# The entry of the MLP: a norm tile's stores moved from ACT's queue to POOL's, and the first raw weights fetched in a step of their own

## The chip, the core and the metric

One core of one Trainium2 chip runs the kernel. The metric is the device time of one execution in microseconds (us), and smaller is better. The engines are named as the profile names them: PE (TensorE, matmuls), ACT (ScalarE), DVE (VectorE), POOL (GpSimd), SP (SyncE, which here only issues DMAs). ACT, SP and POOL each have a queue through which they can start DMAs. An engine takes its own instructions strictly in order, a DMA start among them.

## What is computed

One block of a diffusion transformer over 2048 tokens of 1024 channels: a token mixer (Fourier and neighbourhood attention, gated), and then a dense MLP with 4096 hidden channels. The change touches the place where the second begins.

```python
x = x + g1 * mixed
hx2 = modulate(rms_norm(x, norm2_g[l]), sh2, sc2)
x = x + g2 * sqrelu_mlp(hx2, w_mlp1[l], w_mlp2[l])

def sqrelu_mlp(h, w1, w2):
    a = jax.nn.relu(h @ w1)
    return (a * a) @ w2
```

## The kernel before

Every float32 operand is split into two float16 halves (high and low), and a product of two is three matmuls. The MLP's two matrix products are done as 2x2 block products in the Strassen-Winograd form: seven products of sums of blocks instead of eight. The tokens run in two halves of 1024.

**Up to the MLP.** `out_proj(t, i)` (L1400 on) makes the mixer's output for 128 tokens, adds x, stores the sum to `x1d` through SP's queue and normalises it. `norm_T(t)` (L1420 on) transposes 256 normalised tokens (`tpb`), makes `tm`, and then seven sums of its blocks. For each of the seven, `put` (L1440 on) lets ACT write the high half of a tile `ho` (L1442) and DVE the low half (L1443), and stores it to `hcd` (L1444). The order is 0, 5, 6, 4, 3, 2, 1. There are four `ho` buffers: the fifth, sixth and seventh put wait until the stores of the first three have landed. There are eight tiles t; those of t = 4 to 7 go to `hcd[1]`, which is read when the second half of the tokens begins. Tiles 6 and 7 are stored through ACT's queue, all others through SP's.

**The MLP's operands.** Half 0 reads `hcd[0]` as seven tiles `hc`, 1 MB each, through SP's queue (L1503). Four of them (products 0, 5, 6, 4) are loaded early. The other three (1, 3, 2) live in space (`pr`) that the mixer's output stage (`pg`) held until then; their load is written after `norm_T(7)`.

**The MLP's weights.** They too must be made into seven block sums each, as float16 halves, in DRAM. `prepare` (L383 on) does it for a list of jobs, one job for 256 rows or columns: it fetches a raw weight of 1 MB (`fetch`, L387; here through ACT's queue), and then takes seven steps. Each step has up to one sum on DVE (L423), a high half on ACT (L380) and a low half on DVE (L381), and a store (`flush`, L398; here through POOL's queue). The second step fetches the next raw weight. Eight of the 32 jobs are done far ahead, beside the input projections, by the same generator (`early_blocks`, L367 on; there through SP's queue). The other 24, 168 steps, run beside the MLP's first half. In the loop at the end of the kernel each slot (one product of a unit of the first matrix, or a group of products of the second) adds its cost to `done`, and steps are taken as long as `steps * horizon < done * todo`. `horizon` is the summed cost of the slots within which all must be done: 732, so that a slot of cost 4 takes 4 x 168 / 732 = 0.92 step.

**The MLP's products.** `mlp1(half, f)` yields after each of seven products in the order 0, 5, 6, 4, 1, 3, 2 (`PRODUCTS`). A product is 12 matmuls into one of four PSUM buffers; DVE's sums (`plus`, L1546) and ACT's copies, relus and squares (`acts`, L1550) read it and free the buffer. The first four products of the first unit are written ahead of `norm_T(7)`; the loop starts with the fifth (`if i > 3`).

Within these rules the order of each engine's instructions is set by a scheduler that simulates the program at build time; at run time each engine keeps to that order and waits on semaphores. A DMA of SP's or ACT's queue counts its end on one of eight semaphores, taken in turn by both queues together, and before a DMA is started on such a semaphore the earlier DMA on it must have landed. POOL's queue has eight semaphores of its own.

Of the kernel before, what the change touches and what calls it, by code (L numbers as in the profile page):

```python
# [63 lines left out]
def dit_block(ctx: ExitStack, tc: tile.TileContext, a, out, taps=None, upto=9):  # L64
    nc = tc.nc
    act, dve, pool, pe, sp = nc.scalar, nc.vector, nc.gpsimd, nc.tensor, nc.sync
# [312 lines left out]
    def halve(hi, lo, src, scale):  # L379
        act.activation(hi, src, AF.Copy, scale=scale)  # L380
        dve.scalar_tensor_tensor(out=lo, in0=src, scalar=scale, in1=hi, op0=ALU.mult, op1=ALU.subtract)  # L381

    def prepare(todo, raw_room, sum_room, out_room, n_out, load_, dma):  # L383

        todo, raws, out_, room = list(todo), {}, [], []

        def fetch(n):  # L387
            if n < len(todo):
                kind, f = todo[n]
                raws[n] = t = raw_room(f"raw{kind}_{f}")  # L390
                if kind == 1:
                    load_(t.rearrange("p (k n) -> p k n", k=KT), a["w_mlp1"][0, :, f * 128:(f + 2) * 128].rearrange("(k p) n -> p k n", p=128))
                else:
                    load_(t.rearrange("p (k n) -> p k n", k=2), a["w_mlp2"][0, f * 128:(f + 2) * 128, :].rearrange("(k p) n -> p k n", p=128))

        def flush():
            while out_:
                dma(*out_.pop(0))  # L398

        fetch(0)  # L400
        for n, (kind, f) in enumerate(todo):
            t, nm = raws.pop(n), f"{kind}_{f}"
            if kind == 1:
                t = t.rearrange("p (k n) -> p k n", k=KT)
                b11, b12, b21, b22 = (t[:, 4 * k:4 * k + 4, i * 128:(i + 1) * 128] for i in range(2) for k in range(2))
            else:
                b11, b12, b21, b22 = (t[:, i * 512:(i + 1) * 512] for i in range(4))
            sums = sum_room(f"ws{nm}")
            s3 = sums.rearrange("p (k n) -> p k n", k=4) if kind == 1 else sums

            def put(j, src):

                if j % n_out == 0:
                    flush()
                    room[:] = [out_room(f"wo{nm}_{j}")]
                    end = min(j + n_out, 7)
                    out_.append(((w1d, w2d)[kind - 1][f // 2][j:end].rearrange("c p n -> p c n"), room[0][:, :end - j]))
                o = room[0][:, j % n_out].rearrange("p (o n) -> p o n", o=2)
                d = o.rearrange("p o (k n) -> p o k n", k=4) if kind == 1 else o
                halve(d[:, 0], d[:, 1], src, msc[:, 0:1] if kind == 1 else msc[:, 2:3])  # L420

            def total(o, x, y, op=ALU.subtract):
                dve.tensor_tensor(out=o, in0=x, in1=y, op=op)  # L423
                return o

            if kind == 1:
                order = ((b11, ()), (s3, (b21, b22, ALU.add)), (s3, (s3, b11)), (b12, ()), (b21, (b11, b21)), (b22, ()), (s3, (b12, s3)))
            else:
                order = ((b11, ()), (s3, (b12, b11)), (s3, (b22, s3)), (b22, ()), (b12, (b22, b12)), (b21, ()), (s3, (b21, s3)))
            for j, (o, ops) in enumerate(order):  # L430
                if ops:
                    total(o, *ops)
                put(j, o)
                if j == 0 and n:
                    prepared.add(todo[n - 1])
                if j == 1:
                    fetch(n + 1)
                yield
        flush()
        prepared.add(todo[-1])  # L440
# [979 lines left out]
    def norm_T(t, q_=sp):  # L1420


        tm = pg.tile([128, KT, 2, 128], F32, tag="tm", name=f"tm{t}")
        x0, x1 = (normed.pop((t, i)) for i in range(2))
        for q in range(4):
            tp = tpp.tile([128, 2, 2, 128], F32, tag="tp", name=f"tpb{t}_{q}")
            for j in range(2):
                k = 2 * q + j
                for i, xh in enumerate((x0, x1)):
                    pe.transpose(tp[:, j, i], xh[:, k * 128:(k + 1) * 128], ident)  # L1430
            for j in range(2):
                k = 2 * q + j
                bi, sc = AB2[:, k:k + 1], AB2[:, 8 + k:9 + k]
                if j:
                    dve.tensor_scalar(out=tm[:, k], in0=tp[:, j], scalar1=sc, scalar2=bi, op0=ALU.mult, op1=ALU.add)
                else:
                    act.activation(tm[:, k], tp[:, j], AF.Identity, bias=bi, scale=sc)
        b11, b12, b21, b22 = (tm[:, 4 * k:4 * k + 4, i] for k in range(2) for i in range(2))

        def put(c, src):  # L1440
            o = pg.tile([128, 2, 4, 128], F16, tag="ho", name=f"ho{t}_{c}", bufs=4)
            act.activation(o[:, 0], src, AF.Copy)  # L1442
            dve.tensor_tensor(out=o[:, 1], in0=src, in1=o[:, 0], op=ALU.subtract)  # L1443
            q_.dma_start(hcd[t // 4][c, :, t % 4], o.rearrange("p o k t -> p (o k t)"))  # L1444

        def total(c, x, y, out=None):
            if out is None:
                out = pg.tile([128, 4, 128], F32, tag="hs", name=f"hs{t}_{c}", bufs=2)
            dve.tensor_tensor(out=out, in0=x, in1=y, op=ALU.subtract)
            return out  # L1450

        t1 = total(4, b12, b11)
        t2 = total(5, b22, t1)
        put(0, b11)
        put(5, t2)
        total(6, b22, b12, b12)
        put(6, b12)
        put(4, t1)
        put(3, total(3, b21, t2))
        put(2, b22)  # L1460
        put(1, b21)
# [37 lines left out]
    def load_hc(half, part, then=None):  # L1499
        r = {}  # L1500
        for c in (PRODUCTS[:4], PRODUCTS[4:])[part]:
            r[c] = (pr if part else pl).tile([128, 4, 2, 4, 128], F16, tag=f"hc{c}", name=f"hc{half}_{c}")
            i = sp.dma_start(r[c].rearrange("p s o k t -> p s (o k t)"), hcd[half][c])  # L1503
        if then:

            then[0] = i
        return r
# [11 lines left out]
    def blocks_of(s):  # L1519
        return [s] if s[0] == 1 else [(2, s[1], f, s[3]) for f in s[5]]  # L1520
# [8 lines left out]
    def load_block():  # L1529
        b = next(stream, None)  # L1530
        if b is None:
            return
        kind, half, f, c = b
        while (kind, f) not in prepared:
            next(prep)
        wbs[b] = t = pl.tile([128, 2, 512], F16, tag="wb", name=f"wb{kind}_{half}_{f}_{c}", bufs=RING)
        with tc.issue_after(ring_load[0].ins) if ring_load[0] else nullcontext():
            ring_load[0] = sp.dma_start(t.rearrange("p o n -> p (o n)"), (w1d, w2d)[kind - 1][f // 2][MADE[kind].index(c)])
# [72 lines left out]
    t = NT - 2  # L1611
# [8 lines left out]
    units[0, 0] = mlp1(0, 0)  # L1620
    for _ in range(4):
        next(units[0, 0])
    norm_T(t + 1, act)
    if taps and "x1" in taps:
        sp.dma_start(taps["x1"], x1d)
    for p_ in (pg, tpp):
# [10 lines left out]
    def small(name):  # L1637
        return pr.tile([128, 512], F32, tag="wo", name=name, bufs=5)

    prep = prepare(jobs, lambda n_: pr.tile([128, 2048], F32, tag="raw", name=n_, bufs=2), lambda n_: pr.tile([128, 512], F32, tag="wt", name=n_),  # L1640
                   lambda n_: small(n_).bitcast(F16).rearrange("p (c n) -> p c n", c=1), 1, act.dma_start, pool.dma_start)
    acc, banks = {}, {}
# [80 lines left out]

    todo, steps, done = 7 * len(jobs), 0, 0
    cost = [4 if s[0] == 1 else len(s[5]) for s in slots]
    horizon = sum(cost[:next(i for i, s in enumerate(slots) if s[:4] == (2, 0, NF - GF, 0)) - RING])
    for i, s in enumerate(slots):
        anchors = dict(last)
        if s[0] == 1:
            _, half, f, c = s  # L1730
            if (half, f) not in units:
                units[half, f] = mlp1(half, f)
            if i > 3:
                next(units[half, f])
        else:
            mlp2(*s[1:])
        for b in blocks_of(s):
            if uses[b] == i:
                load_block()
        if s == (1, 0, NF - 2, PRODUCTS[-1]):  # L1740
            hcs[1] = {c_: t_ for part in range(2) for c_, t_ in load_hc(1, part).items()}
        with behind_last(anchors, "dve"), behind_last(anchors, "act"):
            done += cost[i]
            while steps * horizon < done * todo and next(prep, "end") is None:
                steps += 1
# [56 lines left out]
```

## Time and profile before

| | us |
|---|---|
| median of 3 runs | 2702.88 (2701.36 to 2703.93) |
| the profiled execution | 2706.24 |
| its span, first to last instruction | 2704.4 |
| PE busy in it | 2563.6 (95%) |
| DVE, ACT, POOL busy | 1813.9, 1169.9, 462.6 |
| MLP's first product starts at | 1505.8 |
| second matrix's first products start at | 1608.4 |

The profile was taken in the profiled execution; times in it are microseconds from its first instruction. The median of the runs is 3.4 us below that execution. In a timeline, a line tells when a group of like instructions starts, how long the group lasts, how many there are and, in brackets, how long the engine had been idle before and what released it.

### The profile page before, as it was taken

To read this page: it belongs to the slowest core of one execution; us is meant where nothing else is said; L and a number is where in the kernel's file an instruction comes from. 1 tells how busy PE (TensorE), PEld (TensorE's weight loads), DVE (VectorE), ACT (ScalarE), POOL (GpSimd) and SP (SyncE) were. 2 spreads that over 40 slices of the span, in tenths; PEclk is the share of its full clock that TensorE was granted. 3 is DMA by queue.
4 is the path that set the end of the run, shared out by engine and by line. 5 is a ranking of instruction groups with operands and counts; after the bars stand their busy time and mean duration, and the time that the engine had idled before them with its cause. 6 is when DMAs were issued, how large, how long until landed. Compare 5 with 4: busy or idle time off the path is not lost.

```text
span 2704.4 us, 42578 instructions
## 1 busy us (share of the span) xinstructions
PE 2563.6 (95%) x15825; PEld 1564.8 (58%) x15825; DVE 1813.9 (67%) x3636; ACT 1169.9 (43%) x2097; POOL 462.6 (17%) x702
## 2 busy tenths in 40 slices
PE   7899988898999799998999789999999999999999
PEld 5445656766656678887888434444444444444444
DVE  7746975567562588897766596888876743636367
ACT  5623325544231578883444373636352332314050
POOL 1201211012233454531000012121210100000000
PEclk9999989998999899998999899999999999999999
DMA  8576789766353744556667677777766633333334
GB/s 265 148 223 199 216 235 295 259 217 202 102 171 95 191 131 139 143 178 218 218 208 266 216 226 262 230 261 241 252 224 227 209 94 109 94 110 93 112 101 154
DMA packets 344232, 509.36 MB, mean 188 GB/s; under 512 B 48369, under 2 KB 210377, under 8 KB 339673
## 3 DMA queue, kind: packets, MB, share of 16 engines
q1 hardware_dynamic: 294249, 398.11, 47.4%
q0 software_dynamic: 28544, 73.39, 8.0%
q10 hardware_dynamic: 21232, 35.15, 4.0%
q8 instruction: 124, 2.03, 0.3%
q14 instruction: 83, 0.68, 0.1%
HBM read 361.72 MB, written 145.84 MB: 188 GB/s over the span
## 4 chain that ended last, share of the span: by engine, by line
PE 71%; DMA 11%; DVE 10%; ACT 3%; issue 2%; POOL 1%; SPq 1%; ACTq 0%; DVEq 0%; POOLq 0%
PE p L82 21%; PE pm L82 19%; PE ps_g L82 8%; PE po L82 7%; DMA w12m<-in_w_mlp 4%; PE pua L82 3%; PE tp L1271 2%; PE ps_k L82 2%; PE pmf L1209 2%; PE pv L1285 2%; DMA raw<-in_w_mlp 1%; PE sc L1249 1%; PE ps_f L82 1%; DMA vF<-vo_v 1%; DVE wo L381 1%
## 5 line engine op out<-in xcount | busy, mean ns | idle before, releaser
L82 PE MATMUL pm<-hc,wb 128*128 128x512 f16 x2688 | 587.1, 381 | 21.5 <-DMA hc<-hcd 12.0
L82 PE MATMUL p<-wb,a 128*128 128x512 f16 x2688 | 581.8, 379 | 2.7 <-DVE X L1666 1.6
L82 PEld LDWEIGHTS <-wb 128*128 128x128 f16 x2688 | 263.9, 98 | 343.2 <-issue 29.5
L82 PEld LDWEIGHTS <-a 128*128 128x128 f16 x2688 | 262.9, 98 | 320.3 <-issue 3.4
L82 PE MATMUL ps_g<-hx,w_g 128*128 128x512 f16 x1536 | 344.3, 382 | 1.2 <-ACT ot_f L509 1.2
L1546 DVE TENSOR_TENSOR X<-X,p 128x512 f32<-128x512 f32 x280 | 183.8, 682 | 176.1 <-PE p L82 155.3
L82 PEld LDWEIGHTS <-hx 128*128 128x128 f16 x2304 | 228.7, 100 | 49.2 <-issue 9.9
L82 PEld LDWEIGHTS <-w_g 128*128 128x128 f16 x1536 | 151.5, 99 | 173.4 <-issue 6.1
L1546 DVE TENSOR_TENSOR u<-pm,u 128x512 f32<-128x512 f32 x128 | 87.5, 688 | 90.5 <-PE pm L82 88.9
L1037 POOL DMA_DIRECT2D bt<-tT x264 | 132.4, 508 | 77.0 <-DVE ri L1278 58.0
L1258 DVE CUSTOM_DVE_ANT_0 s<-sc,bt,qsc 128x736 f32<-128x736 f32 (+5 forms) x128 | 111.1, 868 | 41.3 <-PE sc L1252 37.8
L380 ACT ACTIVATE wo<-ws,msc 128x512 f16<-128x512 f32 x96 | 68.9, 718 | 152.2 <-DVE ws L423 119.6
L1550 ACT ACTIVATE p<-pm 128x512 f32<-128x512 f32 x32 | 18.9, 589 | 239.4 <-PE pm L82 239.2
L509 ACT ACTIVATE ot_g<-ps_g,usc_g 128x512 f32<-128x512 f32 x64 | 43.7, 684 | 174.8 <-PE ps_g L82 162.4
L1279 DVE SCALAR_TENSOR_TENSOR pL<-tp,pH 128x640 f16<-128x640 f32 (+1 forms) x128 | 112.1, 876 | 6.6 <-ACT pH L1274 6.3
L380 ACT ACTIVATE wo<-raw,msc 128x512 f16<-128x512 f32 x128 | 87.8, 710 | 66.1 <-issue 25.5
L1680 POOL DMA_DIRECT2D xr<-x1d x32 | 17.3, 539 | 570.3 <-DVE X L1546 562.1
L1262 ACT ACTIVATE s<-s,m 128x736 f32<-128x736 f32 (+5 forms) x128 | 104.4, 816 | 13.1 <-DVE m L1258 12.4
L82 PE MATMUL po<-wouH,mH 128*128 128x512 f32 x256 | 101.0, 398 | 7.1 <-DVE ga L1328 7.1
L1271 PE MATMUL tp<-ident,s 128*128 128x128 f32 x704 | 105.0, 283 | 2.1 <-ACT s L1262 2.0
L82 PE MATMUL po<-wouL,mH 128*128 128x512 f32 x256 | 100.2, 393 | 0.0
L82 PE MATMUL po<-wouH,mL 128*128 128x512 f32 x256 | 100.2, 393 | 0.0
(503 smaller groups left out, 4741.4 us busy)
## 6 DMA issues: line engine op xcount, KB each, us to landing
wb<-w1d SPq DMA_DIRECT2D x224, 256.0 KB
wb<-w2d SPq DMA_DIRECT2D x224, 256.0 KB
w12m<-in_w_mlp SPq DMA_DIRECT2D x32, 1024.0 KB
raw<-in_w_mlp ACTq DMA_DIRECT2D x24, 1024.0 KB
w1d<-wo POOLq DMA_DIRECT2D x84, 256.0 KB, 3.8
w2d<-wo POOLq DMA_DIRECT2D x84, 256.0 KB, 3.9
gT<-ot_g SPq DMA_DIRECT2D x64, 256.0 KB
hc<-hcd SPq DMA_DIRECT2D x14, 1024.0 KB
```

What stands on the lines that cost most here:

```text
L82: last_mm[0] = pe.matmul(ps, l, r, start=(start and i == 0), stop=(stop and i == n - 1))
L380: act.activation(hi, src, AF.Copy, scale=scale)
L381: dve.scalar_tensor_tensor(out=lo, in0=src, scalar=scale, in1=hi, op0=ALU.mult, op1=ALU.subtract)
L509: act.activation(o, ps, func, scale=scale)
L1037: load_(t[i * 16:(i + 1) * 16, :, off + j0 * w:off + (j0 + 8) * w], raw(tT[ct], (2 * hp * 15 + dr) * w, [[120 * w, 16], [15 * w, 2], [1, 8 ...
L1209: pe.matmul(ps, l, r, start=(i == 0), stop=(i == len(prods) - 1))
L1258: tail["dve"] = dve.tensor_tensor_reduce(out=s[:, :n], in0=sc, in1=bias, op0=ALU.add, op1=ALU.min, scale=qsc[:, 4:5], scalar=3.0e38, accum ...
L1262: tail["act"] = act.activation(s[:, :n], s[:, :n], AF.Exp, bias=m1[:, 0:1], scale=-1.0, accum_out=m1[:, 1:2])
L1271: tail["pe"] = pe.transpose(tp[:, i * 128:(i + 1) * 128], s[:, o:o + 128], ident)
L1279: tail["dve"] = dve.scalar_tensor_tensor(out=pL[:, :c], in0=tp[:, :c], scalar=PTOP, in1=pH[:, :c], op0=ALU.mult, op1=ALU.subtract)
L1285: tail["pe"] = pe.matmul(pv, p_[:nk, i * 128:(i + 1) * 128], vv[:nk, h2 * 128 + o:h2 * 128 + o + 64], start=(j == 0 and i == 0), stop=(j = ...
L1546: last["dve"] = dve.tensor_tensor(out=o, in0=x, in1=y, op=op)
```

## The change

Three edits. The last `norm_T`'s seven stores are started from POOL's queue instead of ACT's. `prepare` yields once after its first fetch, so that the fetch is a step of its own; that holds for both users of the generator. In the loop, the first eight slots get cost 0, so no step is taken in them (and `horizon` falls by 8 x 4 to 700), and at the fifth slot the generator is called once, which is the fetch of the first raw weight.

```diff
@@ -398,6 +398,7 @@
                 dma(*out_.pop(0))
 
         fetch(0)
+        yield
         for n, (kind, f) in enumerate(todo):
             t, nm = raws.pop(n), f"{kind}_{f}"
             if kind == 1:
@@ -1620,7 +1621,7 @@
     units[0, 0] = mlp1(0, 0)
     for _ in range(4):
         next(units[0, 0])
-    norm_T(t + 1, act)
+    norm_T(t + 1, pool)
     if taps and "x1" in taps:
         sp.dma_start(taps["x1"], x1d)
     for p_ in (pg, tpp):
@@ -1723,8 +1724,11 @@
 
     todo, steps, done = 7 * len(jobs), 0, 0
     cost = [4 if s[0] == 1 else len(s[5]) for s in slots]
+    cost[:8] = [0] * 8
     horizon = sum(cost[:next(i for i, s in enumerate(slots) if s[:4] == (2, 0, NF - GF, 0)) - RING])
     for i, s in enumerate(slots):
+        if i == 4:
+            next(prep)
         anchors = dict(last)
         if s[0] == 1:
             _, half, f, c = s
```

## Rows read from the trace of the kernel before

**Rows 1.** PE's timeline at the entry: start, length, instruction, count, idle before.
```profile
1518.20 1.11 PE L1430 MATMUL tpb<-ident,xh 128*128 128x128 f32 x8 [0.96 <-DVE tm L1435]
1528.80 5.28 PE L82 MATMUL pm<-hc,wb 128*128 128x512 f16 x12 [9.49 <-DMA hc<-hcd]
1535.23 2.75 PE L82 MATMUL pm<-hc,wb 128*128 128x512 f16 x12 [1.16 <-DMA hc<-hcd]
1539.33 5.34 PE L82 MATMUL pm<-hc,wb 128*128 128x512 f16 x24 [1.35 <-DMA hc<-hcd]
1547.68 7.03 PE L82 MATMUL pm<-hc,wb 128*128 128x512 f16 x24 [3.01 <-DVE p L1546]
1555.31 5.34 PE L82 MATMUL pm<-hc,wb 128*128 128x512 f16 x24 [0.61 <-DVE u L1546]
1561.98 2.75 PE L82 MATMUL pm<-hc,wb 128*128 128x512 f16 x12 [1.33 <-DVE u L1546]
1566.91 18.29 PE L82 MATMUL pm<-hc,wb 128*128 128x512 f16 x84 [2.17 <-DVE u L1546]
1605.86 2.75 PE L82 MATMUL pm<-hc,wb 128*128 128x512 f16 x12 [1.64 <-DVE p L1546]
```

**Rows 2.** Stretches: length, busy time by engine, granted PE clock, DMA share, GB/s.
```profile
1519.30:1528.80 9.50, 0.01 (x2) 0.00 (x0) 6.19 (x11) 3.64 (x7) 0.00 (x0) 0.59 0.60 179
1528.80:1547.70 18.90, 13.39 (x49) 5.28 (x49) 5.37 (x9) 3.35 (x6) 0.73 (x2) 0.85 0.99 336
```

**Rows 3.** SP's queue in the timeline, two windows: the DMAs it starts.
```profile
1494.07 12.99 SPq L1412 DMA_DIRECT2D x1d<-x  x2
...
1522.70 0.32 SPq L1503 DMA_DIRECT2D hc<-hcd  x1
```

**Rows 4.** SP's queue, 1440 to 1620: total wait, times, longest.
```profile
SPq L1503 <- DMA hcd<-ho: 23.0, 3, 15.6
```

**Rows 5.** ACT's timeline at the entry, its DMA starts among it.
```profile
1508.33 1.13 ACT L1442 ACTIVATE ho<-tm 128x512 f16<-128x512 f32 x2
...
1520.41 0.33 ACTq L1444 DMA_DIRECT2D hcd<-ho  x1
...
1523.43 1.86 ACTq L1444 DMA_DIRECT2D hcd<-ho  x3
1525.39 0.63 ACT L1442 ACTIVATE ho<-hs 128x512 f16<-128x512 f32 x1 [1.60 <-DVE hs L1449]
1529.53 1.23 ACT L1442 ACTIVATE ho<-tm 128x512 f16<-128x512 f32 x2 [3.52 <-DMA hcd<-ho]
...
1532.17 4.46 ACTq L392 DMA_DIRECT2D raw<-in_w_mlp  x2
```

**Rows 6.** DVE's timeline where the first raw weight lands.
```profile
1544.28 0.69 DVE L423 TENSOR_TENSOR ws<-raw 128x512 f32<-128x512 f32 x1 [6.24 <-DMA raw<-in_w_mlp]
...
1546.94 0.68 DVE L1546 TENSOR_TENSOR p<-pm,p 128x512 f32<-128x512 f32 x1
```

**Rows 7.** DVE in L381, then in L423, one stretch: length, busy, count, clock, DMA.
```profile
1544.20:1566.90 22.70, 6.54 (x9) 0.92 0.93 311
...
1544.20:1566.90 22.70, 4.24 (x7) 0.92 0.93 311
```

**Rows 8.** POOL's timeline (first), then the tile w1d: issue durations (ns), landing.
```profile
1546.66 0.62 POOL L398 DMA_DIRECT2D w1d<-wo  x1 [37.87 <-DVE wo L381]
...
L398 POOL DMA_DIRECT2D w1d<-wo x84: 539/539/623, 1546.7 to 1935.2; - x84
...
DMA to landing us min/median/max: 2.3/3.8/9.6
```

**Rows 9.** A stretch of the second group of units, columns as in rows 2.
```profile
1740.00:1755.00 15.00, 15.00 (x71) 6.77 (x70) 14.57 (x25) 10.49 (x18) 2.71 (x5) 1.00 0.70 230
```

**Rows 10.** Where the early jobs begin: DVE's line, then PE's.
```profile
500.88 0.69 DVE L423 TENSOR_TENSOR ws<-raw 128x512 f32<-128x512 f32 x1 [2.75 <-DMA raw<-in_w_mlp]
...
501.87 0.38 PE L82 MATMUL ps_v<-w_v,hx 128*128 128x256 f16 x2 [2.02 <-ACT vo_v L639]
```

## The prediction

> **What bounds the kernel now.** The views were read in this order. The page says that PE is busy for 95% of the span, so an edit pays only where PE stands still or is slow. PE's timeline around the MLP's entry [rows 1] shows where: after the last transposes, which end at 1518.20 + 1.11 = 1519.31, PE waits 9.49, 1.16 and 1.35 us for the three late `hc` loads (products 1, 3, 2), then 3.01 us for DVE's sum `p`, then 0.61, 1.33 and 2.17 us for DVE's sums `u`. It is also slow twice: 12 matmuls take 5.28 us from 1528.80 where the next 12 take 2.75, and 24 take 7.03 us from 1547.68 where 24 take 5.34 next. The stretches say why: the granted clock falls to 0.59 while PE idles and is 0.85 in the next one [rows 2]. From 1519.31 to the second matrix's products at 1605.86 + 2.75 = 1608.61 are 89.3 us. In them PE has 24 products to do (28 in four units, less the four done before); the 84-matmul line gives 18.29 / 7 = 2.61 us each, so 62.7 us. The entry thus holds 26.6 us that aren't work.
>
> What the three loads wait for is the first question. SP starts its last `x1d` store by 1494.07 + 12.99 = 1507.06, and then waits until 1522.70 for the first load [rows 3]; the waits table puts 15.6 us of it, and 23.0 for all three, down to the `ho` stores [rows 4]. It can't be the `ho` tiles' space: the first load leaves 2.3 us after the start of the tile's first store (1520.41), while buffers of that tile are written again at 1525.39 and 1529.53 [rows 5]. So it is the completion semaphore: eight stand in turn for SP's and ACT's DMAs together, and the loads of products 1, 3 and 2 got those of ACT's stores of sums 0, 5 and 4. The list of the built program before says the same; the only other wait it gives these loads is for the last matmul of `out_proj`, done before the MLP's first product at 1505.8.
>
> **Part 1: the seven stores go to POOL's queue.** Removed from ACT: seven DMA starts. Removed from the shared semaphores: seven stores. The loads then come right behind tile 6's stores in turn and meet DMAs that ended before: ACT wrote buffers of tile 6's first stores again from 1508.33 on, so those had landed [rows 5]. I expect SP to start the three loads at 1507 to 1509. A load alone took 1522.70 to 1528.80, 6.1 us [rows 1, 3]. Three of them one after another end at 1513.3, 1519.4 and 1525.5; together, at the 336 GB/s of the crowded stretch [rows 2], sooner. PE wants them at 1519.3, 1521.9 and 1524.5. I take all three waits as gone: **12.0 us**, bounds 8 (with tile 6's stores and weight loads in the way) to 12. With the idle time goes the low clock: 5.28 - 2.75 = 2.53 and 7.03 - 5.34 = 1.69, **4.2 us**.
>
> Added to POOL: seven starts of 0.54 us, each behind DVE's low half. Nothing waits behind them: POOL has nothing to do until the first weight store, after 37.87 us of idle time [rows 8]. Who does wait are the `ho` buffers: puts 5 to 7 need the first three stores to have landed. A store of the same size through POOL's queue takes 3.8 us to land (2.3 to 9.6) [rows 8]; the ones at 1523.43 on ACT's queue held the put at 1529.53, some 6 us, with a load in flight [rows 5]. At 3.8 the sixth and seventh puts start at about 1527.2 and 1528.
>
> The Trainium skill, SBUF — State Buffer, "SBUF: two separate sides", speaks against this part: POOL writes the descriptors of its DMAs through a port that it shares with DVE and can be locked out while DVE works, and its advice is to use ACT's or SP's queue instead. The rows on weight stores don't show it: 0.54 us per start, with DVE busy 14.57 of 15 us beside five of them [rows 8, 9]. The Trainium skill's page limits the lock to DVE's two-port modes, and no run here shows one.
>
> **Part 2: the first fetch ahead, its blocks eight products later.** ACT now starts two raw fetches at 1532.17, and DVE's first step waits for the landing at 1544.28; the sum `p` that frees PE's next PSUM buffer is queued behind it, at 1546.94 [rows 5, 6]. After the change no step stands in that place. `p` comes after the seventh put: ACT 1528 + 0.63, DVE 0.7, then the fetch's start, one ACT copy and one DVE low half, so done near 1531. PE has done products 1, 3, 2 and the next unit's first by 1519.3 + 4 x 2.61 = 1529.7. The 3.01 us become about 1.2: **1.8 us**, bounds 3.0 (stores at 2.3) to -4 (stores at 9.6). The fetch is started near 1529 and lands near 1535 (6.1 us like the load above), before the first unit's dozen further sums of 0.69 us are through, near 1539; the fetch itself costs nothing then.
>
> The waits of 0.61, 1.33 and 2.17 us, 4.1 in all, fall where DVE carries 9 low halves and 7 sums of `prepare`, 10.8 us of work within 22.7 [rows 1, 7]. By slot 13 the pace rule had asked for 13 steps; now it asks for 6, none of them ahead of the first unit's sums. I take 3 of the 4.1 as gone, **3.0 us**, bounds 0 to 4.1. The later waits (1.64 us at 1605.86 among them) stay.
>
> **Part 3: the pace.** 168 steps over a cost of 700 instead of 732 are 0.96 a slot instead of 0.92. A step is a low half, 6.54 / 9 = 0.73 us, and four of seven have a sum, 4.24 / 7 = 0.61 us: 1.07 us of DVE [rows 7]; 8 x 0.92 = 7.3 steps, 7.9 us of DVE work, move into later units, 0.3 us for each. In the tightest stretch there DVE is busy 14.57 of 15 us while PE isn't held up [rows 9]. So most hides in the slack; when that is used up it is PE's wait. I charge **-0.5 us**, bounds 0 to -7.9.
>
> **Part 4: the extra yield in the early jobs.** It moves all their steps back by one call. At their start DVE waits 2.75 us for the raw weight and PE 2.02 us for ACT [rows 10]; a step later could shed that or put the wait elsewhere. I take 0, bounds -4 to +4, twice that wait of PE's.
>
> Sum: 12.0 + 4.2 + 1.8 + 3.0 - 0.5 = 20.5 us. The profiled execution, 2706.2 us, becomes 2685.7. It lies 3.4 above the median of the runs, so the forecast for the median is 2702.9 - 20.5 = **2682 us**.
>
> **Rivals.** (a) POOL's stores land late, near 9.6 us: the sixth put starts at 1533.0 instead of 1527.2, and `p` moves by the same 5.8 us: 14.7 us gained, 2688. For it: the longest landing; against: the median [rows 8], and that loads pause after 1525. This is how the rule of the Trainium skill's SBUF page would show.
>
> (b) The loads are freed by the stores all the same, whichever queue they use, since the space is handed over by a tile's last use. First store landed at 1520.4 + 3.8 = 1524.2, load at 1530.3: the 12.0 and the first clock loss stay and grow by 1.5. Left are 1.7 + 1.8 + 3.0 - 0.5 - 1.5 = 4.5 us: 2698. For it: the waits table alone [rows 4]; against: the order of stores and load [rows 3, 5].
>
> (c) The slower one: the whole of the old space must be free, the seventh store landed, before a load starts. Seventh put at 1528, low half at 1529.4, start 0.54, landing 3.8: 1533.7 where it was 1522.70. PE starts again at 1539.8, 11.0 later than now; the 6.0 us of the other terms (1.7 + 1.8 + 3.0 - 0.5) come back: 5 us slower, 2708. It decides as soon as that landing is past 1528.7. With landings of 9.6 it is 11 us, 2714. Against: before, the first load left with six stores still to come [rows 3, 5].
>
> (d) The fetch isn't ahead: ACT reaches it at 1529 behind the puts, 3 us earlier than now. With the steps put off it decides nothing; it is in the sum.
>
> **How the numbers follow.** Forecast 0.72, (a) 0.12, (b) 0.10, (c) 0.06. The forecast's own range: its terms at their good ends with +4 from part 4 are 12.0 + 4.2 + 3.0 + 4.1 + 4 = 27.3 us, 2675.6; with the loads at 8 and the pace at -3 it is 14.0, 2689. To hold 8 in 10 it takes in (a), and to leave room for unknown orders on the way to (b) I go to 2694. This kernel's measurement can tell about 0.2%, 5.4 us: forecast and (a) are faster, (b) lies within, (c) at the edge of slower or past it. Faster 0.86, same 0.09, slower 0.05.
>
> **What would show it.** Right: SP starts the three `hc` loads by 1510; PE's wait behind the transposes is under 1 us, the clock stays at 1.00 there; the first `p` runs near 1531; the second matrix starts near 1588. Wrong: loads still behind stores; DVE waiting for a raw weight in the first two units; new PE waits on DVE in the second and third groups of units of more than 3 us; a shift of more than 4 us already before 1500.

## The result and the profile after

| | before | after |
|---|---|---|
| median, runs taken beside each other | 2702.12 (2691.66 to 2703.93, 4 runs) | 2672.72 (2669.02 to 2675.8, 4 runs) |
| the profiled execution | 2706.24 | 2669.02 |
| its span | 2704.4 | 2666.8 |
| MLP's first product starts at | 1505.8 | 1489.9 |
| second matrix's first products start at | 1608.4 | 1571.9 |
| between these two: the **entry** | 102.6 | 82.0 |
| from there to the end of the span | 1096.0 | 1094.9 |

The ratio is 0.9898 (95%: 0.988 to 0.9917): the kernel is faster by 1.0%. The forecast was 2682 with a range of 2675 to 2694; the time lies 9.3 us below the one and 2.3 us below the other. Between the two profiled executions lie 37.2 us (37.6 in their spans), and the table says where: 20.6 us at the entry, 1.1 us behind it, which makes 21.7 where 20.5 were forecast, and 15.9 us ahead of the MLP's first product, where none were. Two executions of the kernel before, of 6221 and 15061 us, are left out of every median below.

PE's timeline at the entry after the change answers to [rows 1] (start, length, instruction, count, idle before and its releaser; lines of the changed kernel stand one further down):

```profile
1502.22 1.11 PE L1431 MATMUL tpb<-ident,xh 128*128 128x128 f32 x8 [0.96 <-DVE tm L1436]
1503.17 10.52 PE L82 MATMUL pm<-hc,wb 128*128 128x512 f16 x48
1514.13 2.75 PE L82 MATMUL pm<-hc,wb 128*128 128x512 f16 x12 [0.44 <-DVE p L1547]
1517.53 7.93 PE L82 MATMUL pm<-hc,wb 128*128 128x512 f16 x36 [0.65 <-DVE u L1547]
1525.69 2.75 PE L82 MATMUL pm<-hc,wb 128*128 128x512 f16 x12 [0.23 <-DVE u L1547]
1529.96 18.29 PE L82 MATMUL pm<-hc,wb 128*128 128x512 f16 x84 [1.52 <-DVE u L1547]
1549.37 18.29 PE L82 MATMUL pm<-hc,wb 128*128 128x512 f16 x84 [1.13 <-DVE u L1547]
1569.29 2.75 PE L82 MATMUL pm<-hc,wb 128*128 128x512 f16 x12 [1.63 <-DVE p L1547]
```

Behind the transposes 48 matmuls follow without a gap: the three waits for `hc` (9.49, 1.16, 1.35 us) are gone, and so are the slow lines. What is left of PE's waits behind the transposes are six for DVE, 5.6 us together.

SP's queue, POOL and ACT in the same stretch, each from its own timeline; they answer to [rows 3], [rows 8] and [rows 5]:

```profile
1490.77 0.32 SPq L1413 DMA_DIRECT2D x1d<-x  x1
1491.25 1.85 SPq L1504 DMA_DIRECT2D hc<-hcd  x3
```

```profile
1504.70 0.62 POOL L1445 DMA_DIRECT2D hcd<-ho  x1 [11.89 <-DVE ho L1444]
1507.99 1.63 POOL L1445 DMA_DIRECT2D hcd<-ho  x3 [2.67 <-DVE ho L1444]
```

```profile
1510.65 0.63 ACT L1443 ACTIVATE ho<-tm 128x512 f16<-128x512 f32 x1 [0.58 <-DMA hcd<-ho]
1511.52 0.63 ACT L1443 ACTIVATE ho<-tm 128x512 f16<-128x512 f32 x1 [0.24 <-DMA hcd<-ho]
1511.54 0.42 ACTq L392 DMA_DIRECT2D raw<-in_w_mlp  x1
```

The loads now start at 1491.25, right behind the last `x1d` store and 13 us before the first of the seven stores. The sixth and seventh puts wait 0.58 and 0.24 us for POOL's stores to land, and the raw fetch follows them. The stretches (length, PE, PEld, DVE, ACT, POOL busy with counts, granted PE clock, DMA share, GB/s), beside [rows 2]:

```profile
1502.20:1514.10 11.90, 11.47 (x56) 5.61 (x57) 9.87 (x16) 6.51 (x12) 3.89 (x7) 1.00 0.80 271
1490.00:1572.00 82.00, 75.45 (x354) 34.59 (x352) 66.43 (x108) 50.80 (x87) 13.12 (x24) 1.00 0.81 270
```

The granted clock is 1.00, the 2.4 GHz level, through the whole entry.

### The profile page after: what moved, and what is told of

The parts are those of the page before. It is cut to its first block, busy times and chain, and to the rows that moved or that the text cites. A ratio compares the mean times of both kernels' runs of the same rounds, so it can differ in the third digit from the quotient of the medians.

```text
span 2666.8 us, 42588 instructions
## 1 busy us (share of the span) xinstructions
PE 2553.8 (96%) x15825; PEld 1559.9 (58%) x15825; DVE 1814.4 (68%) x3636; ACT 1169.4 (44%) x2097; POOL 470.0 (18%) x709
## 4 chain that ended last, share of the span: by engine, by line
PE 72%; DVE 10%; DMA 9%; ACT 3%; issue 3%; SPq 2%; POOL 1%; ACTq 0%; DVEq 0%; POOLq 0%
PE p L82 21%; PE pm L82 18%; PE ps_g L82 8%; PE po L82 6%; DMA w12m<-in_w_mlp 4%; PE pua L82 3%; PE tp L1272 2%; PE ps_k L82 2%; PE pmf L1210 2%; PE pv L1286 2%; SPq L182 1%; PE sc L1250 1%; PE ps_f L82 1%; PE sc L1253 1%; DVE wo L381 1%
## 5 line engine op out<-in xcount | busy, mean ns | idle before, releaser
L1263 ACT ACTIVATE s<-s,m 128x736 f32<-128x736 f32 (+5 forms) x128 | 104.4, 816 | 13.0 <-DVE m L1259 12.4
```

Of the source, the lines that this page charges most:

```text
L1263: tail["act"] = act.activation(s[:, :n], s[:, :n], AF.Exp, bias=m1[:, 0:1], scale=-1.0, accum_out=m1[:, 1:2])
```

## The experiments

The kernels ran in three groups, each group with its own runs of the kernel before. "Entry" is the stretch named in the table above, read from PE's timeline of each profiled execution.

| kernel | median us (range; runs) | before beside it | ratio (95%) | entry us |
|---|---|---|---|---|
| e1_early_only | 2694.44 (2690.05 to 2700.76; 11) | 2697.11 (21) | 0.9986 (0.9974 to 0.9997) | 102.7 |
| e2_entry_only | 2676.35 (2672.46 to 2679.97; 5) | 2697.11 | 0.9926 (0.9912 to 0.9939) | 82.0 |
| e3_stores_only | 2685.15 (2683.26 to 2688.02; 4) | 2697.11 | 0.9954 (0.994 to 0.9968) | 91.7 |
| e5_loads_pool | 2691.64 (2685.63 to 2698.82; 10) | 2697.11 | 0.998 (0.9968 to 0.9992) | 97.0 |
| e4_steps_only | 2683.77 (2680.73 to 2688.2; 9) | 2697.77 (20) | 0.9954 (0.9941 to 0.9968) | 90.5 |
| e6_early_two | 2700.19 (2689.77 to 2706.35; 12) | 2697.77 | 1.0007 (0.9993 to 1.0022) | 102.8 |
| a1_changed | 2676.43 (2674.2 to 2677.54; 6) | 2697.77 | 0.9924 (0.9908 to 0.994) | 82.0 |
| e7_zero14 | 2670.88 (2669.96 to 2679.33; 6) | 2697.77 | 0.9913 (0.9894 to 0.9931) | 78.8 |
| p4_with | 2672.55 (2670.23 to 2675.46; 4) | 2699.42 (17) | 0.9899 (0.9884 to 0.9915) | 82.1 |
| p4_without | 2675.07 (2672.86 to 2677.92; 4) | 2699.42 | 0.9909 (0.9893 to 0.9924) | 82.2 |
| p4_alone | 2696.1 (2691.85 to 2702.01; 12) | 2699.42 | 0.9989 (0.9979 to 0.9999) | 103.0 |

### The stores alone

```diff
-    norm_T(t + 1, act)
+    norm_T(t + 1, pool)
```

> Only the last norm tile's stores go through POOL's queue; the first block's steps still come in the loop's first slots. Theory: the three late hc loads start within 3 us of the MLP's first product and PE no longer waits for them (12.0 us and 2.5 us of slow clock gone), but DVE's sum p still stands behind a step that waits for the raw weight, which lands some 6 us after ACT has started its fetch; of the 14.5 us about 5 to 6 come back as PE's wait for p (8 to 9 us instead of 3.0). 8 to 10 us less than before. Rival (the two parts add up): 16 us less, p's wait stays at 3.

Measured: 12.4 us by the ratio, 10.9 at the entry, a little more than the 8 to 10 expected; PE's wait for `p` came out as expected. Lines from SP's and PE's timelines, then from the waits at the entry (waiting engine, line, releaser: total, times, longest):

```profile
1496.11 3.06 SPq L1503 DMA_DIRECT2D hc<-hcd  x3
```

```profile
1508.04 10.52 PE L82 MATMUL pm<-hc,wb 128*128 128x512 f16 x48
1527.30 6.83 PE L82 MATMUL pm<-hc,wb 128*128 128x512 f16 x24 [8.73 <-DVE p L1546]
```

```profile
DVE ws L423 <- DMA raw<-in_w_mlp: 4.9, 1, 4.9
```

The loads are free 1.4 us after the MLP's first product (1494.73), and no wait for `hc` is left. But PE, no longer late, comes to the sum `p` too early: DVE has a step of `prepare` ahead of it and stands 4.9 us for the raw weight. PE's wait for `p` grows from 3.01 to 8.73 us, and the low clock comes back behind it (24 matmuls in 6.83 us). Of the 16.2 us that part 1 set free, this edit alone keeps about 11.

### The loads through another queue, the stores left where they were

```diff
-            i = sp.dma_start(r[c].rearrange("p s o k t -> p s (o k t)"), hcd[half][c])
+            i = (pool if part and not half else sp).dma_start(r[c].rearrange("p s o k t -> p s (o k t)"), hcd[half][c])
```

> Before, with one edit: the three late hc loads of the first half go through POOL's queue; the last norm tile's stores stay on ACT's. Theory (the loads wait for nothing but the semaphores that SP's and ACT's DMAs share): they start about 3 us after the MLP's first product although the stores are where they were, PE's 12.0 us behind the transposes are gone, and the time falls by 6 to 9 us, since DVE's wait for the raw weight stays. Rival (the stores themselves hold the loads, by space or by traffic on ACT's queue): the loads start 15 us or more after the first product, and the time is within 2 us of before.

Measured: 5.4 us by the ratio, 5.6 at the entry, just under the 6 to 9 expected. POOL's timeline, then PE's:

```profile
1494.34 0.63 POOL L1503 DMA_DIRECT2D hc<-hcd  x1
1495.15 1.09 POOL L1503 DMA_DIRECT2D hc<-hcd  x2 [0.18 <-issue]
```

```profile
1504.63 10.52 PE L82 MATMUL pm<-hc,wb 128*128 128x512 f16 x48
1530.03 12.50 PE L82 MATMUL pm<-hc,wb 128*128 128x512 f16 x48 [14.88 <-DVE p L1546]
```

This tells the semaphore from the space. The stores of the last tile still go through ACT's queue, the loads write to the same place, and they start 3.0 us after the MLP's first product (1491.32), long before any of those stores. So neither the stores nor the space held them, but the semaphore that SP's loads shared in turn with ACT's stores. The packed trace of before also has the semaphores' numbers, which the views above leave out: ahead of the three loads SP waits on 102, 103 and 105, and these are the ones on which ACT's stores started at 1520.41, 1523.43 and 1524.63 count their ends. For the time it does less than the stores' move: the wait for `p` is 14.88 us here, as long as the 15.0 us that PE waited before for the loads and `p` together, and what is won is mostly the later sums and the clock. DVE first stands 4.73 us for the raw weight and then has seven operations of `prepare` ahead of `p`, which starts at 1529.30; before the change and in e3_stores_only there were four.

### The steps alone

```diff
-        fetch(0)
+        fetch(0); yield from [None] * ahead
...
-                   ..., 1, act.dma_start, pool.dma_start)
+                   ..., 1, act.dma_start, pool.dma_start, 1)
...
-    cost = [4 if s[0] == 1 else len(s[5]) for s in slots]
+    cost = [4 if s[0] == 1 else len(s[5]) for s in slots]; cost[:8] = [0] * 8
...
-        anchors = dict(last)
+        anchors = dict(last) if i != 4 else (next(prep), dict(last))[1]
```

The cuts are marked with "...". The generator's new argument, `ahead`, is the number of yields after its first fetch; for the early jobs it stays at none.

> Only the MLP's steps: the first fetch ahead, no step in the first eight slots; the last norm tile's stores stay on ACT's queue. Theory: PE's waits for the three hc loads (12.0 us) and the first slow clock (2.5 us) stay; p no longer stands behind a raw weight (3.0 us and the second slow clock of 1.7 us gone) and about 3 of the 4.1 us of waits for u go. 6 to 8 us less than before. Rival (the steps only matter once the loads are early): within 3 us of before.

Measured: 12.4 us by the ratio, 12.1 at the entry, more than I had looked for. PE's timeline:

```profile
1516.36 5.16 PE L82 MATMUL pm<-hc,wb 128*128 128x512 f16 x12 [9.92 <-DMA hc<-hcd]
1522.44 2.75 PE L82 MATMUL pm<-hc,wb 128*128 128x512 f16 x12 [0.92 <-DMA hc<-hcd]
1526.19 57.44 PE L82 MATMUL pm<-hc,wb 128*128 128x512 f16 x264 [1.00 <-DMA hc<-hcd]
```

The three waits for the loads stay as before, 11.8 us. After them PE runs 264 matmuls, 22 products, without a stop: DVE, free of steps while PE stood still, starts the first `p` at 1521.66, 4.5 us before PE has its third load, and stays ahead for the rest of the entry. So the two parts aren't a sum of their own prices. Alone they bring 10.9 and 12.1 us, together 20.6: the stores' move needs the other edit to keep its gain, and the other edit loses some of its own when PE no longer stands still first.

### Both, without the early jobs' yield, and the whole change again

> All of the change but the early jobs' yield. Theory: 20 to 21 us less than before (ratio 0.9922 to 0.9926), 82 us from the MLP's first product to the second matrix's first. Rival (the early yield gives nothing): the whole difference of the changed kernel, 27 to 29 us less (ratio 0.9892 to 0.9900).

> The changed kernel again, beside the runs of the kernel before of this call. Theory: its two parts add up: 20.0 us from the entry and 3.8 from the early jobs, 23 to 25 us less than before, ratio 0.9907 to 0.9917. Rival: the parts help each other, 27 us or more.

The first has the diffs of the two experiments above together, the second is the changed kernel. Both entries are 82.0 us, wait by wait that of the first profile. The ratios, 0.9926 and 0.9924, are from different groups. The first, 20.0 us, is within what was expected. The second, 20.5 us, misses its 23 to 25: set against each other across the groups, these two leave only some 0.5 us for the yield in the early jobs.

### The yield in the early jobs

```diff
-                            2, sp.dma_start, sp.dma_start)
+                            2, sp.dma_start, sp.dma_start, 1)
```

> Only the early jobs (beside the input projections) yield once after their first fetch; the MLP's steps and the norm tile's stores are as before. Theory: the gain beyond the entry's 20.6 us comes from this yield, which changes the order of DVE's, ACT's and SP's work between 582 and 685 us; PE's waits there fall from 10.6 to 6.4 us. 5 to 6 us less than before, ratio 0.9978 to 0.9982, and the MLP's entry as before (102.6 us from its first product to the second matrix). Rival: the order is worth nothing, and what the changed kernel gained beyond the entry is variation between executions: within 2 us of before, ratio 0.9993 to 1.0007.

> The early jobs yield twice after their first fetch; everything else as before. If a later start of their steps is what helps in that stage, two yields give at least what one gave (3.8 us) : 4 to 8 us less than before. If one yield only happened to give a better order of the scheduler's, two may give anything: 0 us, or a loss.

> The whole change, beside the same kernel without the extra yield in the early jobs, on one chip. If the yield is worth the 3.8 us that it showed alone, this kernel is 3 to 5 us below the other one; if that was scatter, the two medians lie within 2 us. The entry (MLP's first product to the second matrix's) takes 82.0 us in both.

> The change without the early jobs' yield: 3 to 5 us above the whole change if the yield is worth what it showed alone, within 2 us of it if not. Entry 82.0 us; PE's waits between 560 and 700 us add up to about 8.7 us, against 6.4 to 8.5 with the yield.

> The yield alone, once more: 0.9986 (3.8 us faster) if the first measurement was right, 0.999 to 1.001 if it was scatter. Entry 102.6 us, as before the change.

e6_early_two passes 2 where e1_early_only passes 1; p4_with, p4_without and p4_alone are the kernels of a1_changed, e2_entry_only and e1_early_only, run beside each other. Alone, the yield gave 0.9986 and 0.9989, 3.8 and 3.0 us, both intervals just short of 1; the first is less than the 5 to 6 expected. With the rest, it is 2.5 us between the medians of p4_with and p4_without (4 runs each, ranges that overlap), between the two answers expected. Two yields give nothing: 1.0007.

PE's waits from 560 to 700 us, where the early jobs run, in p4_without and then in p4_with:

```profile
PE pu_g L487 <- DVE usc_k L488: 3.2, 1, 3.2
PE ps_k L82 <- DVE qn_k L570: 2.8, 3, 1.8
PE tq_k L596 <- DVE sL_k L607: 2.3, 1, 2.3
PE pvm L835 <- DVE vsc L833: 1.2, 1, 1.2
```

```profile
PE pu_g L487 <- DVE usc_k L488: 4.2, 1, 4.2
PE ps_k0c L82 <- DVE qn_k L570: 2.9, 1, 2.9
PE pvm L835 <- DVE vsc L833: 0.3, 1, 0.3
```

9.5 us without the yield, 7.4 with it. In the six profiles of kernels with one yield (after, e1, a1, e7, p4_with, p4_alone) these waits are 6.4 to 8.5 us; in the six without (before, e2 to e5, p4_without) they are 8.5 to 12.0, 2.3 us more in the mean. What tells the two sets apart better than these sums is the stretch in which PE's own order of instructions differs. It begins and ends with the same instructions in every kernel with one yield or none; here they are in before and then in after:

```profile
595.96 2.78 PE L82 MATMUL ps_k<-w_k,hx 128*128 128x256 f16 x24
675.63 0.38 PE L596 MATMUL tq_k<-ident,qr_k 128*128 128x128 f32 x2
```

```profile
586.82 2.78 PE L82 MATMUL ps_k<-w_k,hx 128*128 128x256 f16 x24
659.83 0.38 PE L597 MATMUL tq_k<-ident,qr_k 128*128 128x128 f32 x2
```

From the start of the first to the start of the second it takes 73.0 to 75.1 us in the six profiles with one yield and 75.7 to 79.7 in the six without: 74.0 and 76.9 in the mean, 2.9 us apart, and the two sets don't overlap. So the yield does act there. Among PE's waits it is those for DVE's work on the keys (`qn_k`, `sL_k`) that change: PE waits 1.8 to 3.5 us for `sL_k` in each of the six without the yield, and in one of the six with it, 1.2 us. Why this order of DVE's work is the better one isn't shown. From that point to the MLP's first product the profiles lie 8 us apart (825.8 to 833.7), more than the yield brings, so what is left of it at the end is known only from the times: 2 to 4 us within groups, some 0.5 across them. With two yields the order already differs from 522 us on. This stretch then takes 72.1 us, the shortest of all, but the 409 PE instructions ahead of it take 58.4, where the other twelve profiles have 53.7 to 55.9, and the gain is lost again.

### Fourteen slots without steps

```diff
-    cost[:8] = [0] * 8
+    ...; cost[:14] = [0] * 14
```

> The changed kernel with no step in the first 14 slots instead of 8; the pace becomes 168 steps over 676. Theory (the waits for u of the second unit come from steps in its slots): 1 to 2 us of 3.2 us of waits go, and the denser pace gives 0.5 to 1 back: 24 to 26 us less than before. Rival (the denser pace decides, DVE being over 95% busy in the second group's units): 20 to 22 us less than before, with new waits for DVE in the second and third groups of units.

PE's timeline at the entry, and then PE's waits from the second matrix's first product to the end:

```profile
1526.85 2.75 PE L82 MATMUL pm<-hc,wb 128*128 128x512 f16 x12 [0.71 <-DVE p L1546]
1530.25 46.78 PE L82 MATMUL pm<-hc,wb 128*128 128x512 f16 x216 [0.65 <-DVE u L1546]
1578.51 2.75 PE L82 MATMUL pm<-hc,wb 128*128 128x512 f16 x12 [1.48 <-DVE p L1546]
```

```profile
PE p L82 <- DVE X L1666: 2.4, 1, 2.4
PE p L82 <- DVE X L1546: 1.1, 2, 0.6
```

The entry falls to 78.8 us, and the waits for `u` shrink to one: they were DVE's steps. The waits of the second matrix for `X` are 3.5 us where the changed kernel has 2.1, so about half is given back. The ratio, 23.5 us, lies between the theory's 24 to 26 and the rival's 20 to 22. The median is 5.5 us below that of a1_changed beside it, but the ranges and the intervals (0.9894 to 0.9931 and 0.9908 to 0.994) overlap: no version beat the changed kernel by more than the scatter.

### The kernel before, run again

In the three groups the kernel before has 58 runs: 2690.4 to 2704.33, mean and median 2698.1 and 2698.2. The three runs that the forecast started from (2701.36 to 2703.93) lie in the top quarter of this spread, the profiled execution, 2706.24, lies above it, and the fourth run, beside the changed kernel, took 2691.66. The groups ran on three chips, with means of 2697.5 to 2699.3; whether the first three runs were high by chance or by their chip isn't shown. The changed kernel's 14 runs have a mean of 2674.1. The difference, **24 us**, is the best value for the change; by the three ratios it is 27.6, 20.5 and 27.3 us.

## Why the prediction was wrong

**The sum for the entry and what follows held: 20.5 forecast, 20.6 + 1.1 measured.** By its terms:

| term | forecast | measured |
|---|---|---|
| part 1: the waits for `hc` | 12.0 | 12.0, none left |
| part 1: the slow clock | 4.2 | 4.2, clock 1.00 throughout |
| part 2: the wait for `p` | 1.8 | 3.01 - 0.44 = 2.6 |
| part 2: the waits for `u` | 3.0 | 4.11 - (0.65 + 0.23 + 1.52) = 1.7 |
| part 2: the later waits at the entry | 0 | (0.73 + 1.64) - (1.13 + 1.63) = -0.4 |
| part 3: the pace, after the entry | -0.5 | +1.1: 1094.9 us where it was 1096.0 |

The five terms of the entry add up to 20.1 of its 20.6 us; the rest stands in no single wait. Part 1 came out as worked out. That the whole sum is off by only 1.2 us is in part luck: the four small terms missed by 0.4 to 1.6 us each, in both directions. Nor are the parts what each edit brings alone: part 1's 16.2 us hold only with part 2 beside it, and alone it brought 10.9.

The signs named beforehand answer the same way, counted from the MLP's first product since that came earlier. The loads start 1.4 us after it (forecast 1 to 4, 1507 to 1510 less 1505.8). The first `p` starts 23.5 us after it (1513.39 in DVE's timeline; forecast 25). The second matrix starts 82.0 us after it (forecast 1588 - 1505.8 = 82.2). In part 2, POOL's stores landed sooner than the 3.8 us taken from [rows 8]: the first two of the three started from 1507.99 on released the puts at 1510.65 and 1511.52, after some 3 us each. And the waits for `u` were over-sized: fewer steps do run there, but some still do, and e7_zero14 shows that all but one of those waits go only when none do. The pace cost nothing: the stretch behind the entry is 1094.9 to 1095.0 us in every profile of the whole change with eight slots put off, 1096.4 us with fourteen.

**Part 4 failed: it was taken as 0.** It is worth 2 to 4 us, by two measurements alone and one beside the rest, and 2.9 us in the stretch where PE's order changes; only the comparison across groups gives less. It lay within the bounds of -4 to +4 that [rows 10] gave, but the place was wrong. The row is from the first step of the early jobs, at 500 us, where the order of every engine is the same before and after. What changed is how DVE's steps stand among its work on the keys, between 587 and 692 us. From 560 to 700 us the kernel before has six waits of PE for DVE, 12.0 us together, and the prediction has no row from there.

**The last step of the sum failed: 2702.9 - 20.5.** The median of three runs was taken as the kernel's time, but 58 others put it at 2698.1: 4.8 us lower, more than all of part 4. The rest adds up: 2698.1 - 21.7 is 2676.4, and the nine runs without the early yield (e2_entry_only and p4_without) have a mean of 2676.1; less 2 to 4 for the yield it is 2672.4 to 2674.4, and the mean of 14 runs is 2674.1. The range missed for the same reason. Its low end, 2702.9 - 27.3, had each term of the change at its good end, but nothing for the starting point; from 2698.1 the same terms reach 2670.8. The chances of faster, 0.86, did not depend on it.

**The 15.9 us ahead of the MLP are mostly no effect of the change.** The sign "a shift of more than 4 us already before 1500" did appear, and the scatter is most of its answer. The instructions of the two kernels stand in the same order on every engine until 582 us, and by then the changed kernel's execution is already some 9 us ahead. The stretch that the yield reorders brings another 6.7 us, 79.7 to 73.0, because it sets the longest of the six without the yield against one of the shortest of the six with it; 2.9 of that is the difference of their means. Behind it hardly anything is added, 0.2 us. In the six profiles with one yield the MLP's first product starts at 1489.9 to 1502.3 (the changed kernel, run again, at 1498.4 and 1496.3), 1495.3 in the mean; in the six without it at 1491.3 to 1505.8, 1496.2 in the mean. The two shown in the table above are the ends: one is the earliest of those with it, the other the latest of those without. The two profiles of the one kernel, after and a1_changed, are 8.5 us apart in time (2669.02 and 2677.54), and their first products 8.5 us: all of it lies ahead of the MLP. Stretches of before and then of after, columns as above:

```profile
350.00:480.00 130.00, 107.34 (x741) 75.58 (x739) 80.20 (x192) 54.64 (x106) 20.82 (x20) 0.92 0.87 269
480.00:700.00 220.00, 199.28 (x1524) 151.25 (x1522) 146.33 (x369) 103.45 (x182) 29.20 (x28) 0.97 0.69 223
```

```profile
350.00:480.00 130.00, 109.76 (x787) 78.16 (x785) 81.63 (x194) 59.14 (x112) 19.70 (x19) 0.95 0.89 284
480.00:700.00 220.00, 208.44 (x1590) 157.12 (x1589) 154.35 (x395) 101.76 (x183) 33.30 (x31) 0.98 0.67 217
```

From 350 to 480 us, where both have the same order of instructions, the one execution moved 269 GB/s and the other 284. What sets this rate in an execution stays open.

**The rivals.** (a), stores that land late, did not come: ACT waits 0.82 us in all for them, and the landings of `hcd` are 2.6 to 7.0 us. (b) and (c), loads that wait for the stores or for the whole old space, are excluded by SP's line: the loads start 13 us before the first store. e5_loads_pool excludes them a second way, with the stores still on ACT. (d) was as said: the fetch starts 0.02 us after the seventh put and holds up nothing.

The rule that spoke against part 1 (the Trainium skill, SBUF — State Buffer, "SBUF: two separate sides": while DVE runs an operation in a two-port mode, POOL is locked out and can't write the descriptors of its DMAs, so these belong on ACT's or SP's queue) shows no effect here. The seven starts on POOL took 0.54 us each (one 0.62) with DVE busy 9.87 of 11.9 us beside them. This doesn't test the rule, since no row tells in which mode an operation of DVE ran. Moving the stores the other way, onto POOL, gained 10.9 us at the entry alone, by freeing the semaphores that the loads shared.

## What to carry to other kernels

When a DMA start waits for a transfer that it has nothing to do with, ask which completion semaphore the two share: here moving either of them to another queue ended the wait. But look first at what is queued behind, because the wait moved on to DVE's sum until its queue was cleared as well. Price edits that act on one chain together, since alone they brought 10.9 and 12.1 us and together 20.6. Before a forecast in microseconds is tied to a median, ask how far runs of that kernel lie apart, and give the starting point a term in the range; and read the stretch around every user of a shared helper that is edited, however far it is from the place that the edit is meant for.

## What was not expected of the hardware

One kernel's executions spread over 14 us (2690.4 to 2704.33, 58 runs), 0.5%, and in two profiles of one kernel the whole difference of 8.5 us arose ahead of the MLP; the changed kernel's entry was 82.0 to 82.2 us in every profile of it, with the early jobs' yield or without.

Less idle time ahead can cost an engine later: in e4_steps_only PE stands 11.8 us for the loads and then runs 57 us without a stop, while in the changed kernel, which has no such pause, six short waits for DVE add up to 5.6 us over the same products.
